# Routing of a mixture of experts: rows for the gathers made behind the choice of experts, a second index list moved forward, weights' high parts cast earlier

## The chip, the cores and the metric

The kernel runs on one core of one Trainium2 chip, in one launch. The metric is the time of one execution on the device in microseconds (us); less is better. A core has five engines that work side by side, each through its own instructions in order: TensorE (PE in the profile, with its weight loads as PEld), VectorE (DVE), ScalarE (ACT), GpSimd (POOL) and SyncE (SP), which here only issues DMA transfers. They wait for each other through semaphores.

## The reference

One decoder layer on 512 tokens of 1024 channels. An attention and a recurrent mixer come first; then a mixture of 16 experts, which is where the change lies:

```python
u = layer_norm(x) * (1.0 + sc_f) + sh_f
grp_prob = softmax(t @ w_grp + b_grp)              # 4 groups, top 1
sel_logits = ...                                   # 4 experts of that group
top_w, top_idx = top_k(softmax(sel_logits), 2)     # top 2
...
for e in range(16):
    h = silu(t @ w_e_gate[e]) * (t @ w_e_up[e])
    y = y + comb[:, e:e + 1] * (h @ w_e_down[e])
x = layer_norm(alpha * x + (1.0 + gt_f) * y, ln2_g, ln2_b)
```

All is float32. `t` is `u` with one row for each token.

## The kernel before, in words

**Blocks.** The 512 tokens are four blocks of 128 (t = 0 to 3). Each block's attention output is projected (`out_half`, L938, in halves h: `oh(t, h)` is its products, `oe(t, h)` its addition to x on DVE, L945) and goes through two layer norms, `out_ln` (L969), in five steps `L[t][0..4]`:

- `L[t][0]`: mean on DVE (L951), squares on ACT (L957), one scaling pass on DVE in two halves (L978), the reciprocal root on POOL (L962, L326).
- `L[t][1]`: the pass with that root (L984), which gives x of the next residual.
- `L[t][2]`: mean, squares and root of the second norm.
- `L[t][3]`: u2's first pass, (x + mean) × scale row, two DVE instructions on 128x512 (L994).
- `L[t][4]`: u2's second pass, × root + shift row (L998), and on POOL's queue the DMA that writes the block's rows to `u2d` in device memory (L999). Experts gather their tokens from there.

**Logits.** They don't need u2. `RT[t]` (L1005) transposes x on PE, `RE[t]` (L1010) copies it out on ACT, `RL[t]` (L1030) multiplies by the folded routing weights (L1034), and `RN[t]` (L1037) applies both roots on DVE (L1040, L1041). `SX[t]` (L1017) scales x on ACT and writes it to `x2d` by a DMA on ACT's queue.

**Choice and positions.** `R[0]` to `R[2]` (L1189 to L1208) choose the group, the first and the second expert in small DVE steps over all four blocks. `R[3]` (L1210) makes the mask `mkb` (L1212), counts every token's place in its expert by small products on PE, and makes `posb` (L1219). `R[4]` counts each expert's tokens. `OR`, `PT`, `SP_` and `PP` (L1266, L1559 to L1570) order the experts by load; the order goes to SP for the later weight loads.

**The first expert.** Its tokens are not gathered: `FO` (L1536) makes a one-hot matrix `oh0` from `posb`, `FM(t)` (L1540) multiplies block t of u2 with it on PE, sixteen 128x128 products in the trace, and `FX` (L1551) splits the sum into a high and a low part, cast on ACT (L97) and subtracted on DVE (L98). `IX[p]` (L1525, L1359) makes another expert's index list, by a one-hot on DVE (L1379) and a product with it on PE (L1317), and starts its gather on POOL's queue (L1333).

**Parts.** An expert's weights come in twelve tiles of 512 KB, four each of gate, up and down. For experts with over 64 places each tile is split: high part by a cast on ACT (L811), low part by a subtraction on DVE or, for every second tile of four, POOL (L812). Three products (L101 to L103) stand for one. `e_half` (L1466) does the gate or the up half, 24 products of 128x512. `pre_split(g)` (L1162) splits the first expert's gate tile g ahead of that. There are four pairs of buffers for high and low parts.

**Idle work.** `K(n)` (L1119) and `KR(name, n)` (L1127) issue n products on PE whose result nobody reads; a `KR` waits for the tile named. Each float32 product of this sort is two records in the trace.

**Order.** `TAIL` (L39) is a list written out by hand. Each entry issues its instructions on all engines it uses, so the list is the order of every engine's queue in this stretch. What follows the list is ordered by the framework's scheduler, which may let it pass steps of the list on DVE, ACT and POOL; PE's and SP's order is always the written one. `ahead(n)` (L1060) issues n weight loads on SP's queue. Such a load waits until its buffer is free; eight of these buffers hold the four blocks of x and the rows g1, b1, scf and shf before, so they come free with `SX` and with the last uses in `L[t][0]`, `L[t][1]`, `L[t][3]` and `L[t][4]`.

Of the kernel before, what the change touches and what calls it, by code (L numbers as in the profile page):

```python
# [8 lines left out]
F32 = mybir.dt.float32  # L9
# [10 lines left out]
S = 512  # L20
# [27 lines left out]
def block_kernel(ctx, tc, x, c, w_ada, b_ada, w_in, b_f, conv_w, conv_b, w_rg, b_rg, w_ig, b_ig,  # L48
# [3 lines left out]
    V, A, G, T, SP = nc.vector, nc.scalar, nc.gpsimd, nc.tensor, nc.sync  # L52
# [654 lines left out]
    FR = [fold_shift, fold_scale(scfT), fold_mean, fold_b1, fold_scale(vt[:, 0:8]), fold_mean]  # L707
# [34 lines left out]
    def GW(n, k, eng):  # L742
        return lambda: eng.tensor_mul(st["wo" + n][k], st["wo" + n][k], gtm)
# [50 lines left out]
    wq = {}  # L794
# [14 lines left out]
    def e_split(r, eng=None):  # L809
        hl = hilo(list(r.shape))  # L810
        A.copy(hl[0], r)  # L811
        (eng or V).tensor_sub(hl[1], r, hl[0].bitcast(F32))  # L812
        return hl
# [246 lines left out]
    def ahead(n):  # L1060
        return lambda: load_next(n)
# [7 lines left out]
    L = {t: out_ln(t) for t in range(NT)}  # L1069
    SS = [lambda t=t: att_ss(t) for t in range(NT)]  # L1070
# [48 lines left out]
    def K(n):  # L1119
        def f_():  # L1120
            p = ps([128, 128])
            for _ in range(n):
                T.matmul(p, ident, ident, start=True, stop=True)
# [14 lines left out]
    E5 = ahead(NRW)  # L1138
# [740 lines left out]
```

## Time and profile before

| | us |
|---|---|
| median of 3 runs | 660.27 |
| lowest and highest | 658.4, 661.78 |
| profiled execution | 662.26 |
| its span, first to last instruction | 660.6 |
| PE busy in it | 601.3 |
| DVE, ACT, POOL busy | 459.8, 322.5, 187.7 |

The profile has one execution. A row of a timeline reads: start, duration of the stretch, engine, line, operation, what it writes and reads, the shapes, how many instructions were merged, and in brackets how long the engine had been idle and whose result ended that. A row of the table by stretch has the stretch, its length, busy time and number of instructions of PE, PEld, DVE, ACT and POOL, then the granted share of TensorE's clock (1.00 is full), the DMA engines' share and GB/s. Times count from the span's start. The routing lies between about 285 and 321 us; the experts follow, and a last layer norm from 626 on.

### The profile page before, as it was taken

How to read it: one execution, taken by the hardware profiler on the slowest of the kernel's cores; microseconds unless marked ns; L12 is line 12 of the kernel's file. 1: busy time of each engine (PE TensorE's matmuls, PEld its weight loads, DVE VectorE, ACT ScalarE, POOL GpSimd, SP SyncE). 2: the span in 40 equal slices, each digit the busy share in tenths (PEclk: the TensorE clock that was granted, in tenths of full speed). 3: DMA queues.
4: the chain of work that ended last, by engine and by line, in shares of the span. 5: the costliest groups of instructions: out<-in, count | busy, mean ns of one | idle time of the engine just before them, and what ended most of it. 6: DMA issues, size and time to landing. Idle time of an engine off the chain costs nothing. (4 is left out here: it accounts for less than half of the span.)

```text
span 660.6 us, 10240 instructions
## 1 busy us (share of the span) xinstructions
PE 601.3 (91%) x3545; PEld 442.5 (67%) x3545; DVE 459.8 (70%) x739; ACT 322.5 (49%) x508; POOL 187.7 (28%) x191
## 2 busy tenths in 40 slices
PE   4898999999999999989799999999999999999960
PEld 0556868767886888879577776566767677676440
DVE  6757879844655677896789577747677685985185
ACT  0444887343444465742666455345536364552170
POOL 8700004000000000330255334344436344443023
PEclk9899999999999999987989999999999899999885
DMA  9996045977367123556699969799989999699503
GB/s 314 342 261 219 5 160 183 292 232 223 96 222 262 60 70 122 200 214 223 205 362 382 376 207 381 233 350 332 353 280 370 369 377 360 224 388 384 203 18 113
DMA packets 90578, 164.61 MB, mean 249 GB/s; under 512 B 9321, under 2 KB 29913, under 8 KB 90524
## 3 DMA queue, kind: packets, MB, share of 16 engines
q1 hardware_dynamic: 83796, 149.02, 64.6%
q0 software_dynamic: 5024, 10.70, 6.2%
q10 hardware_dynamic: 1704, 4.21, 1.7%
q8 instruction: 29, 0.48, 0.3%
q14 instruction: 25, 0.20, 0.1%
HBM read 155.54 MB, written 12.39 MB: 254 GB/s over the span
## 5 line engine op out<-in xcount | busy, mean ns | idle before, releaser
L812 DVE TENSOR_TENSOR wlo<-er,whi 128x1024 fp32r<-128x1024 f32 x91 | 145.1, 1612 | 31.6 <-ACT whi L811 30.0
L811 ACT CAST whi<-er 128x1024 fp32r<-128x1024 f32 x120 | 125.3, 1049 | 73.3 <-PE ps L103 64.2
L812 POOL TENSOR_TENSOR wlo<-er,whi 128x1024 fp32r<-128x1024 f32 x29 | 74.3, 2563 | 78.5 <-ACT whi L811 78.3
L101 PE MATMUL ps<-uh,whi 128*128 128x512 f32 x160 | 64.4, 403 | 0.0
L102 PE MATMUL ps<-wlo,xth 128*128 128x512 f32 x144 | 58.5, 406 | 5.7 <-POOL wlo L812 4.1
L103 PE MATMUL ps<-uh,wlo 128*128 128x512 f32 x160 | 62.6, 391 | 0.0
L102 PE MATMUL ps<-ul,whi 128*128 128x512 f32 x160 | 62.4, 390 | 0.0
L1418 PE MATMUL ps<-er,xT 128*64 128x256 f32 x512 | 60.3, 389 | 0.0
L101 PE MATMUL ps<-whi,xth 128*128 128x512 f32 x144 | 59.4, 412 | 0.0
L103 PE MATMUL ps<-whi,xtl 128*128 128x512 f32 x144 | 58.2, 404 | 1.2 <-DVE xtl L98 1.2
L1418 PEld LDWEIGHTS ps<-er,xT 128*64 128x64 f32 x512 | 36.0, 140 | 20.8 <-issue 5.0
L326 POOL TENSOR_TENSOR rA<-rA,nhalf 128x1 f32<-128x1 f32 x4 | 2.2, 548 | 157.4 <-DVE rA L917 157.4
L101 PEld LDWEIGHTS ps<-uh,whi 128*128 128x128 f32 x160 | 30.1, 188 | 11.5 <-issue 3.9
L102 PEld LDWEIGHTS ps<-wlo,xth 128*128 128x128 f32 x144 | 27.7, 192 | 13.5 <-POOL wlo L812 5.8
L358 DVE TENSOR_TENSOR wlo<-wi,whi 128x1024 fp32r<-128x1024 f32 x20 | 25.5, 1277 | 15.3 <-ACT whi L357 15.3
L357 ACT CAST whi<-wi 128x1024 fp32r<-128x1024 f32 x20 | 21.0, 1048 | 28.8 <-DMA wi<-in_w_in_dram 17.0
L103 PEld LDWEIGHTS ps<-uh,wlo 128*128 128x128 f32 x160 | 30.0, 188 | 6.9 <-DVE wlo L358 0.5
L102 PEld LDWEIGHTS ps<-ul,whi 128*128 128x128 f32 x160 | 30.1, 188 | 6.4 <-issue 0.5
L102 PE MATMUL ps<-wlo,hth 128*128 128x512 f32 x80 | 31.9, 398 | 2.5 <-DVE wlo L812 2.5
L103 PEld LDWEIGHTS ps<-whi,xtl 128*128 128x128 f32 x144 | 27.9, 194 | 8.1 <-DVE xtl L98 1.6
L101 PE MATMUL ps<-whi,hth 128*128 128x512 f32 x80 | 32.4, 405 | 0.0
L101 PEld LDWEIGHTS ps<-whi,xth 128*128 128x128 f32 x144 | 27.9, 194 | 5.8
(416 smaller groups left out, 1266.5 us busy)
## 6 DMA issues: line engine op xcount, KB each, us to landing
er<-in_w_e_gate_dram SPq DMA_DIRECT2D x64, 512.0 KB, 8.2
er<-in_w_e_up_dram SPq DMA_DIRECT2D x64, 512.0 KB, 10.6
er<-in_w_e_down_dram SPq DMA_DIRECT2D x64, 512.0 KB, 10.9
wa<-in_w_ada_dram SPq DMA_DIRECT2D x44, 512.0 KB, 8.6
wi<-in_w_in_dram SPq DMA_DIRECT2D x20, 512.0 KB, 4.9
wo<-in_w_out_dram SPq DMA_DIRECT2D x8, 512.0 KB, 5.0
wa<-in_w_ada_dram ACTq DMA_DIRECT2D x4, 512.0 KB
x<-in_x_dram SPq DMA_DIRECT2D x4, 512.0 KB, 6.0
```

The costliest lines, as they stand in the source:

```text
L101: T.matmul(o, l[0], r[0], start=start, stop=False)
L102: T.matmul(o, l[0], r[1], start=False, stop=False)
L103: T.matmul(o, l[1], r[0], start=False, stop=stop)
L326: G.tensor_tensor(dst, src, nhalf[:, 0:n], op=OP.pow)
L357: A.copy(hl[0], r)
L358: V.tensor_sub(hl[1], r, hl[0].bitcast(F32))
L811: A.copy(hl[0], r)
L812: (eng or V).tensor_sub(hl[1], r, hl[0].bitcast(F32))
L1418: T.matmul(p[64 * h:64 * h + 64, :], xT[:, k, :], ws[w0 + k // 2][:, k % 2, h * 256:(h + 1) * 256], start=k == 0, stop=k == 7)
```

## The change

Nothing is computed differently; the list is reordered, `pre_split` is cut in two, and the idle products are redistributed.

- `L[3][4]`, `L[2][3]`, `L[1][3]` and `L[0][3]` move: the first from before `RT[1]` to between `R[2]` and `R[3]`, the others to behind `FO`, each shortly in front of its own second pass.
- `RE[0]` moves in front of `L[1][2]`, `SX[2]` behind `SP_`.
- `K(10)` becomes `K(6)` in front of `RT[0]` and `K(6)` behind `L[0][2]`; `KR` 5 and 5 become 3 and 2.
- `IX[1]` moves from behind `FX` to in front of `FM(0)`.
- `pre_split(g)` becomes `PA(g)`, the cast on ACT, and `PB(g)`, the subtraction on DVE. `PA(0)` to `PA(2)` go among the choice and the positions, `PA(3)` in front of `FX`; `PB(0)` in front of `FM(0)`, the others behind `FX`.
- `SX[1]` and `SX[0]`, which stood in front of the weights `WM`, go to the very end.

The list from the first difference on, broken into lines here:

```diff
-    RN[3], L[3][4], oh(0, 0), RT[1], RE[1], L[1][1], L[2][3], oh(0, 1), RL[2], oe(0, 0), oe(0, 1), L[0][0],
-    RT[0], RL[1], L[1][2], RE[0], RN[2], L[1][3], L[0][1], RL[0], L[0][2], K(10), SX[3], RN[1], L[0][3], SX[2], RN[0],
-    ahead(3), R[0], KR("em", 5), R[1], KR("oh1", 5), R[2], R[3], FO, L[2][4], R[4], FM(3), IX[0], OR, FM(2), L[1][4],
-    PT, SP_, FM(1), L[0][4], PP, FM(0), pre_split(0), FX, IX[1], pre_split(1), SX[1], SX[0], WM, pre_split(2), pre_split(3),
+    RN[3], oh(0, 0), RT[1], RE[1], L[1][1], oh(0, 1), RL[2], oe(0, 0), oe(0, 1), L[0][0], K(6),
+    RT[0], RL[1], RE[0], L[1][2], RN[2], L[0][1], RL[0], L[0][2], K(6), SX[3], RN[1], RN[0], PA(0),
+    ahead(3), R[0], KR("em", 3), PA(1), R[1], KR("oh1", 2), R[2], L[3][4], R[3], FO, L[2][3], R[4], FM(3), L[2][4], IX[0], OR,
+    PA(2), FM(2), L[1][3], L[1][4], PT, SP_, SX[2], FM(1), L[0][3], L[0][4], PP, IX[1], PB(0), FM(0), PA(3),
+    FX, PB(1), PB(2), WM, PB(3), SX[1], SX[0],
```
```diff
-    def pre_split(g):
-        return lambda: hl0.append(e_split(wq[0][g]))
+    def PA(g):
+        def f_():
+            hl0.append(hilo(list(wq[0][g].shape)))
+            A.copy(hl0[g][0], wq[0][g])
+        return f_
+
+    def PB(g):
+        return lambda: V.tensor_sub(hl0[g][1], wq[0][g], hl0[g][0].bitcast(F32))
```

More of the change, by code (lines that the diff above doesn't have):

```diff
@@ L39, in TAIL @@
 def TAIL(d):
-    (S_, N_, T_, PV_, oh, oe, lo, L, SS, RT, RE, RL, RN, FR, FO, FM, FX, AL, AC, G, V, K, KR, SX, open_e1, open_e3, ahead, pre_split, pj, w_ahead, AU, LW, GW, FW, XA, E5, RW, scsh_rows, R, IX, OR, PT, SP_, PP, WM) = (d[k] for k in ("S_", "N_", "T_", "PV_", "oh", "oe", "lo", "L", "SS", "RT", "RE", "RL", "RN", "FR", "FO", "FM", "FX", "AL", "AC", "G", "V", "K", "KR", "SX", "open_e1", "open_e3", "ahead", "pre_split", "pj", "w_ahead", "AU", "LW", "GW", "FW", "XA", "E5", "RW", "scsh_rows", "R", "IX", "OR", "PT", "SP_", "PP", "WM"))
+    (S_, N_, T_, PV_, oh, oe, lo, L, SS, RT, RE, RL, RN, FR, FO, FM, FX, AL, AC, G, V, K, KR, SX, open_e1, open_e3, ahead, PA, PB, pj, w_ahead, AU, LW, GW, FW, XA, E5, RW, scsh_rows, R, IX, OR, PT, SP_, PP, WM) = (d[k] for k in ("S_", "N_", "T_", "PV_", "oh", "oe", "lo", "L", "SS", "RT", "RE", "RL", "RN", "FR", "FO", "FM", "FX", "AL", "AC", "G", "V", "K", "KR", "SX", "open_e1", "open_e3", "ahead", "PA", "PB", "pj", "w_ahead", "AU", "LW", "GW", "FW", "XA", "E5", "RW", "scsh_rows", "R", "IX", "OR", "PT", "SP_", "PP", "WM"))
@@ L41, in TAIL @@
     S, N, T, PV, le = S_, N_, T_, PV_, oe
     return [
-        AL, AL, pj(1, 0), AC, AC, AL, AL, pj(1, 1), AC, AC, T[0], S[1], N[1], AU[6], pj(2, 0), LW["L"], AL, GW("L", 0, V), GW("L", 1, V), FW["L"][0], pj(2, 1), AL, T[1], PV[0], S[2], AU[7], N[2], AC, AC, FW["L"][1], GW("L", 2, V), AL, pj(3, 0), AU[8], FW["L"][2], GW("L", 3, V), AL, pj(3, 1), AC, AC, AU[9], open_e1, T[2], S[3], N[3], PV[1], S[4], FW["L"][3], AL, AL, AL, AL, PV[2], T[3], N[4], RW[0], lo(0, 1), AC, AC, PV[3], LW["A"], scsh_rows, FR[0], FR[1], XA[0], XA[2], lo(0, 0), AC, AC, GW("A", 0, V), lo(1, 0), FR[2], le(0, 0), le(0, 1), XA[1], S[5], T[4], N[5], GW("A", 1, V), S[6], lo(2, 1), PV[4], RW[1], FR[3], FR[4], lo(2, 0), GW("A", 2, V), GW("A", 3, V), le(1, 0), AU[10], lo(1, 1), FR[5], le(1, 1), XA[3], S[7], T[5], N[6], SS[3], le(2, 1), S[8], PV[5], lo(3, 0), T[6], N[7], le(2, 0), AU[11], lo(3, 1), FW["A"][0], FW["A"][1], FW["A"][2], FW["A"][3], le(3, 0), T[7], E5, N[8], PV[6], S[9], le(3, 1), oh(3, 0), oh(3, 1), T[8], oe(3, 0), PV[7], N[9], S[10], T[9], N[10], PV[8], oe(3, 1), SS[2], oh(2, 1), oh(2, 0), L[3][0], T[10], RT[3], oe(2, 0), RE[3], PV[9], L[3][1], PV[10], RL[3], SS[1], oe(2, 1), open_e3, ahead(4), oh(1, 0), L[3][2], L[2][0], SS[0], RT[2], RE[2], L[3][3], L[2][1], oh(1, 1), oe(1, 0), oe(1, 1), L[2][2], L[1][0], RN[3], L[3][4], oh(0, 0), RT[1], RE[1], L[1][1], L[2][3], oh(0, 1), RL[2], oe(0, 0), oe(0, 1), L[0][0], RT[0], RL[1], L[1][2], RE[0], RN[2], L[1][3], L[0][1], RL[0], L[0][2], K(10), SX[3], RN[1], L[0][3], SX[2], RN[0], ahead(3), R[0], KR("em", 5), R[1], KR("oh1", 5), R[2], R[3], FO, L[2][4], R[4], FM(3), IX[0], OR, FM(2), L[1][4], PT, SP_, FM(1), L[0][4], PP, FM(0), pre_split(0), FX, IX[1], pre_split(1), SX[1], SX[0], WM, pre_split(2), pre_split(3),
@@ new lines, in TAIL @@
+        AL, AL, pj(1, 0), AC, AC, AL, AL, pj(1, 1), AC, AC, T[0], S[1], N[1], AU[6], pj(2, 0), LW["L"], AL, GW("L", 0, V), GW("L", 1, V), FW["L"][0], pj(2, 1), AL, T[1], PV[0], S[2], AU[7], N[2], AC, AC, FW["L"][1], GW("L", 2, V), AL, pj(3, 0), AU[8], FW["L"][2], GW("L", 3, V), AL, pj(3, 1), AC, AC, AU[9], open_e1, T[2], S[3], N[3], PV[1], S[4], FW["L"][3], AL, AL, AL, AL, PV[2], T[3], N[4], RW[0], lo(0, 1), AC, AC, PV[3], LW["A"], scsh_rows, FR[0], FR[1], XA[0], XA[2], lo(0, 0), AC, AC, GW("A", 0, V), lo(1, 0), FR[2], le(0, 0), le(0, 1), XA[1], S[5], T[4], N[5], GW("A", 1, V), S[6], lo(2, 1), PV[4], RW[1], FR[3], FR[4], lo(2, 0), GW("A", 2, V), GW("A", 3, V), le(1, 0), AU[10], lo(1, 1), FR[5], le(1, 1), XA[3], S[7], T[5], N[6], SS[3], le(2, 1), S[8], PV[5], lo(3, 0), T[6], N[7], le(2, 0), AU[11], lo(3, 1), FW["A"][0], FW["A"][1], FW["A"][2], FW["A"][3], le(3, 0), T[7], E5, N[8], PV[6], S[9], le(3, 1), oh(3, 0), oh(3, 1), T[8], oe(3, 0), PV[7], N[9], S[10], T[9], N[10], PV[8], oe(3, 1), SS[2], oh(2, 1), oh(2, 0), L[3][0], T[10], RT[3], oe(2, 0), RE[3], PV[9], L[3][1], PV[10], RL[3], SS[1], oe(2, 1), open_e3, ahead(4), oh(1, 0), L[3][2], L[2][0], SS[0], RT[2], RE[2], L[3][3], L[2][1], oh(1, 1), oe(1, 0), oe(1, 1), L[2][2], L[1][0], RN[3], oh(0, 0), RT[1], RE[1], L[1][1], oh(0, 1), RL[2], oe(0, 0), oe(0, 1), L[0][0], K(6), RT[0], RL[1], RE[0], L[1][2], RN[2], L[0][1], RL[0], L[0][2], K(6), SX[3], RN[1], RN[0], PA(0), ahead(3), R[0], KR("em", 3), PA(1), R[1], KR("oh1", 2), R[2], L[3][4], R[3], FO, L[2][3], R[4], FM(3), L[2][4], IX[0], OR, PA(2), FM(2), L[1][3], L[1][4], PT, SP_, SX[2], FM(1), L[0][3], L[0][4], PP, IX[1], PB(0), FM(0), PA(3), FX, PB(1), PB(2), WM, PB(3), SX[1], SX[0],
```

## The prediction

> **What bounds the kernel now.** I read the page first, then a table of busy time by stretch, then each engine's timeline between 285 and 336 us, which is all that the change touches.
>
> ```profile
> span 660.6 us, 10240 instructions
> ...
> PE 601.3 (91%) x3545; PEld 442.5 (67%) x3545; DVE 459.8 (70%) x739; ACT 322.5 (49%) x508; POOL 187.7 (28%) x191
> ```
> ```profile
> sum 335.00, PE 300.80 PEld 210.88 DVE 233.57 ACT 164.47 POOL 136.36; mean PE 18.80 PEld 13.18 DVE 14.60 ACT 10.28 POOL 8.52
> ```
>
> From 326 us on PE is busy 300.8 of 335.0 us, and the last 35 of these are the closing normalisation. The experts are PE work, so what the routing stretch in front of them gives up should reach the end nearly whole. That stretch is a chain of short steps:
>
> ```profile
> 288.37 0.75 DVE L984 SCALAR_TENSOR_TENSOR xt<-xg,rs,b 128x512 f32<-128x512 f32 x1 [0.44 <-POOL rs L326]
> ...
> 289.72 1.41 DVE L994 SCALAR_TENSOR_TENSOR u<-xt,nmu,scf 128x512 f32<-128x512 f32 x2
> 291.05 0.74 DVE L945 SCALAR_TENSOR_TENSOR xt<-ps,rA,xt 128x512 f32<-128x512 f32 x1
> ...
> 294.63 1.41 DVE L994 SCALAR_TENSOR_TENSOR u<-xt,nmu,scf 128x512 f32<-128x512 f32 x2
> 295.96 0.75 DVE L984 SCALAR_TENSOR_TENSOR xt<-xg,rs,b 128x512 f32<-128x512 f32 x1
> ...
> 300.37 0.24 DVE L1040 SCALAR_TENSOR_TENSOR lg<-ps,rs,b1w 128x20 f32<-128x20 f32 x1 [0.92 <-PE ps L1034]
> 300.72 0.24 DVE L1041 SCALAR_TENSOR_TENSOR lg<-lg,rs,brow 128x20 f32<-128x20 f32 x1
> ...
> 305.11 0.22 DVE L1212 TENSOR_TENSOR mkb<-e1o,e2o 128x64 bf16<-128x64 f32 x1
> 307.95 0.23 DVE L1219 SCALAR_TENSOR_TENSOR posb<-ps,mkb 128x64 bf16<-128x64 f32 x1 [2.62 <-PE ps L1217]
> 308.21 0.69 DVE L1538 TENSOR_TENSOR oh<-iota1b,posb 128x512 f32<-128x512 bf16 x1
> ```
> ```profile
> 287.82 1.85 PE L1034 MATMUL ps<-wr,yT 128*128 128x20 f32 x16
> 291.85 1.83 PE L1008 MATMUL ps<-ident,xt 128*128 128x128 f32 x8 [2.18 <-DVE xt L945]
> 293.48 6.86 PE L1034 MATMUL ps<-wr,yT 128*128 128x20 f32 x32
> 300.17 4.61 PE L1123 MATMUL ps<-ident 128*128 128x128 f32 x20
> ...
> 307.50 0.21 PE L1215 MATMUL ps<-mkb,utrib 128*128 128x16 bf16 x2
> ...
> 315.75 1.06 PE L1297 MATMUL ps<-pm,sT 16*128 16x16 f32 x8
> 316.74 2.05 PE L1548 MATMUL ps<-oh,u 128*128 128x128 f32 x16
> 320.79 0.35 PE L1317 MATMUL ps<-cidx,oh 128*128 128x1 bf16 x8 [2.00 <-DVE oh L1379]
> 321.00 0.48 PE L101 MATMUL ps<-whi,x0h 128*128 128x512 f32 x1
> ...
> 330.36 0.48 PE L101 MATMUL ps<-whi,x0h 128*128 128x512 f32 x1
> ...
> 335.79 0.40 PE L103 MATMUL ps<-whi,x0l 128*128 128x512 f32 x1
> ```
> ```profile
> 293.00:295.00 2.00, 2.00 (x12) 2.00 (x11) 1.96 (x6) 1.65 (x3) 0.74 (x2) 0.50 0.00 0
> ```
>
> See first the clock. Sixteen logit products took 1.85 us (0.116 each) at 288, thirty-two took 6.86 us (0.214 each) at 293: after PE's 2.18 us pause the granted clock is 0.50 (last row, third column from the end). The ten unused products of K (20 records) run at that clock too, 0.23 us each, and keep PE's queue full until 307.5: posb waits 2.62 us behind them, although mkb is there at 305.33.
>
> **The change part by part.** *The passes ahead of the choice.* Four pairs of L994/L998 leave DVE. Block 3's L998 frees nothing: the next step waited 0.44 us for POOL already. Block 2's L994 stood right in front of the last output halves: 291.05 − 289.72 = 1.33 us. Block 1's L994 stood in front of block 0's second step, whose POOL root was there at 294.98:
>
> ```profile
> 294.42 0.56 POOL L326 TENSOR_TENSOR rs<-vs,nhalf 128x1 f32<-128x1 f32 x1
> ...
> 299.58 0.55 POOL L326 TENSOR_TENSOR rs<-vs,nhalf 128x1 f32<-128x1 f32 x1
> ```
>
> so it cost 295.96 − 294.98, about 0.9. Block 0's L994 lay in front of a wait for PE: nothing. The last logits need L1041, which needs the root at 300.13 and ran at 300.72, because L1040 had waited for slow PE products. The new K(6) stands between products that end at 289.67 and transposes that can start near 290.5: twelve records of 0.13 (2.05/16) are 1.5 us, so PE doesn't pause, and the logits keep 0.116. Then the root is what ends last: 0.5 more. Sum 1.33 + 0.9 + 0.5 = 2.7: the choice begins at 298.3 instead of 301.0. If the clock falls all the same, the two sets of products from about 293.0 end at 299.9 and only 0.4 is left. I take 2.7, as K fills the pause that stands in front of the fall.
>
> *The choice and the positions.* From 300.96 to mkb at 305.11 is 4.1 us of small steps; block 3's L998 now stands in front of mkb, 1.33: mkb at 303.7, done 303.9. The product itself takes 307.95 − 307.50 = 0.45, and PE is now free for it, since K's second half ends near 297.5 (first K to 291.2, transposes about 1.1, twice 1.85, second K 1.5) and KR's ten records are short. posb at 304.4 instead of 307.95: 3.5 gained.
>
> *From the positions to the first product.* Six passes now lie here that lay ahead.
>
> ```profile
> 311.30 0.14 DVE L1268 COPY cntT<-ps 16x1 f32<-16x1 f32 x1
> ...
> 312.17 1.39 DVE L998 SCALAR_TENSOR_TENSOR u<-u,rs,shf 128x512 f32<-128x512 f32 x2
> ...
> 316.85 0.22 DVE L1568 CAST posb<-ps 128x56 bf16<-128x56 f32 x1 [1.48 <-PE ps L1297]
> ...
> 319.16 0.23 DVE L1365 TENSOR_SCALAR posc<-posP 128x4 bf16<-128x4 f32 x2
> 319.44 0.69 DVE L98 TENSOR_TENSOR x0l<-ps,x0h 128x512 fp32r<-128x512 f32 x1
> ...
> 322.45 0.17 DVE L1233 TENSOR_TENSOR gd<-lg,gm 128x16 f32<-128x16 f32 x1
> ...
> 325.86 3.49 DVE L812 TENSOR_TENSOR wlo<-er,whi 128x1024 fp32r<-128x1024 f32 x3
> ```
>
> DVE in order from 304.4: posb and oh0 0.9 (305.3), block 2's two passes 2.7 (308.0), the order of experts 312.17 − 311.30 = 0.9 and an index 0.1 (309.0), block 1's two passes 2.7 (311.7). PE: FM(1) 2.05 (313.8), by-position products and their wait 316.85 − 315.75 = 1.1 (314.9; block 0's two passes, 311.8 to 314.5, hide beside these), two casts 0.4, the second one-hot 0.7 (316.0), its product 0.35, FM(0) 2.05 (318.4). The first product follows at 318.5, not 321.0, as its second index list no longer stands in front with a 2.00 us wait: 2.5.
>
> But the new order leaves PE nearly empty: from 297.5 to 305.4 it has KR's ten records (1.3 us) and the positions (0.5), less than in the stretch in front of the fall at 292. I take the clock as halved when FM(3) begins. FM(3) then needs 4.1 instead of 2.05 (305.4 to 309.5), its index 0.7; if dense work has raised the clock by then, FM(2) ends at 312.2, transposes and spread take 0.8, FM(1) ends at 315.1, and the first product comes at 319.8: 1.2 gained. The Trainium skill (TensorE: Matmul & The Clock Gate, Part 1) has the clock halved after an idle window of about 3.4 us. By it the longest gap here, 2.5 us (301.4 to 303.9), would not halve it and the sum would take 318.5; the trace differs, since 2.18 us between thin products was enough.
>
> *High and low parts.*
>
> ```profile
> 320.25 1.06 ACT L1018 ACTIVATE xt<-xt 128x1024 f32<-128x1024 f32 x1
> ...
> 323.87 0.22 ACT L1235 ACTIVATE gx<-gd 128x16 f32<-128x16 f32 x1 [1.09 <-issue]
> ...
> 324.50 3.87 ACT L811 CAST whi<-er 128x1024 fp32r<-128x1024 f32 x4
> ```
> ```profile
> 328.46 3.14 POOL L812 TENSOR_TENSOR wlo<-er,whi 128x1024 fp32r<-128x1024 f32 x1 [4.94 <-ACT whi L811]
> ```
>
> The four casts (0.97 each) go to times when ACT is idle: free. The first gate half took 321.0 to 330.0, 24 products at 0.236 ((335.79 − 330.36)/23) being 5.7; the rest is waiting for parts. Now the last low part ends it. FX's last subtraction ends 320.13 − 318.79 = 1.3 behind FM(0); two low parts at 1.16 are 2.3; the weights took 325.86 − 322.45 = 3.4, of which 1.1 was ACT busy with x's stores, so 2.3; the last low part 1.2. From FM(0)'s end (319.7 with the halved clock) that makes 326.8, five products 1.2 more: 328.0 instead of 330.0. With the clock full, 326.7.
>
> Then the up half. x's last two stores (3.6 us of ACT, 320.25 to 323.87) now stand behind the weights. Casts of the up weights, issued behind the written order, can pass them: L1365 at 319.16 belongs to a later expert and runs between two steps of the list. If the first two pass, the up half follows at 328.3 and ends 5.7 later at 334.0, against 336.2: **2.2 us gained**, the forecast. If they don't, that is the second rival.
>
> *DMAs.* Block 2's store of x goes out near 312.8, not 301.8, and the rows used as scf and shf come free at 313 and 314.5.
>
> ```profile
> 305.26 10.47 SPq L819 DMA_DIRECT2D er<-in_w_e_down_dram  x3
> ```
> ```profile
> x2d<-xt ACTq DMA_DIRECT2D x4, 512.0 KB, 6.1
> ```
>
> These three slots take the second expert's down weights, issued from 305.3 to 315.7, now near 319 (312.8 + 6.1). They are used five blocks of 24 products behind the first: over 28 us of cover, so nothing; without it, 3 us. The gather of the second list gets its list earlier and waits for block 0's rows at 314.5: nothing. The new wait of PB(0) on DVE has only FX queued behind it, and its cast is long done.
>
> **The rivals.** *Clock kept:* if the KR products hold the clock through, the first product is at 318.5, the gate half ends at 326.7 and the up half near 332.7: 3.5 gained, 656.8. For: six KR records at 299.5 split the gap. Against: the fall at 292. The Trainium skill's page named above gives this case.
>
> *Stores in front of the up casts:* with the written order strict, ACT ends the weights' exponentials near 324.9, the stores at 328.5, the casts at 329.5 and 330.6; POOL's low part takes 3.14 (333.7), and the 17 products behind it 4.0: 337.7, 1.5 later than now, 661.8. It decides once the up casts lie behind both stores.
>
> *Clock down through all one-hot products:* the slower case by more than noise. Four FM at 4.1 with double-length products between them end about 8 us later than counted with the clock full, so the gate half ends near 335, 5 us later than now: 665. It needs three dense FM at half clock without a rise; K raised it in about 3.4 dense us (302.3 to 305.7).
>
> *No effect:* the logits' chain bound by PE anyway (0.4 instead of 2.7) while the stores cost what the earlier parts gain: 660.3.
>
> **How the numbers follow.** The profiled execution took 662.26 us (span 660.6); 2.2 less is 660.1. The median of the runs, 660.27, stands 2.0 below it, so I forecast 658.1. Chances: forecast 0.42, clock kept 0.30, stores in front 0.13, no effect 0.06, clock down 0.09. A measurement of this kernel can tell 0.5% (3.3 us) from no change. The runs before spread over 3.4 us, so a case's median can lie a microsecond or two off. Clock kept, 3.5 us, counts two thirds as faster (0.20), the forecast a third (0.14); clock down is slower (0.09), the rest within: faster 0.34, same 0.57, slower 0.09. The range, 654.8 to 662.0, takes in clock kept with 2 us of spread and the stores' case, and leaves clock down out.
>
> **What would show it.** Choice (L1191) near 298.3; posb near 304.4; first product of the experts between 318.5 and 319.8; the granted clock 0.50 somewhere between 299 and 309; the last gate low part near 326; the first two up casts on ACT ahead of x's last store. Wrong if L1034 still takes 0.21 us each behind K(6), if FM(2) and FM(1) take over 4 us, or if the gain up to the up half's end isn't that of the end.

## The result and the profile after

| | changed kernel | kernel before, beside it | ratio (95% interval) |
|---|---|---|---|
| first comparison, 4 runs each | 668.20 (665.57 to 671.01) | 661.02 (658.4 to 662.54) | 1.0131 (1.0084 to 1.0178) |
| again, as a0 below, 12 runs | 667.56 (665.52 to 669.93) | 660.52 | 1.0095 (1.0064 to 1.0127) |

Medians in us; the ratio is worked out from the single runs and is not the quotient of the medians, from which it can differ by some 0.3%. In the ratios, here and below, runs over 1.5% above the fastest of their kernel are left out (of the kernels below one of e9's, 1490.65 us, and two of f3's, 662.75 and 663.23), while the medians have them in. The change makes the kernel about 1% slower: by a0's twelve runs 7.0 us by the medians and 6.3 by the ratio, where 2.2 us of gain were forecast and the range ended at 662.0.

The profiled execution took 671.01 us. Its page begins:

```profile
span 669.3 us, 10225 instructions
...
PE 603.7 (90%) x3539; PEld 443.7 (66%) x3539; DVE 460.0 (69%) x739; ACT 322.5 (48%) x508; POOL 181.5 (27%) x191
```

PE is busy 2.4 us longer than before, the span is 8.7 us longer: PE mostly waits more.

To lay two kernels beside each other, a point upstream of the change is needed. The ninth load of expert weights on SP's queue serves, first in the kernel before, then in the changed one:

```profile
270.95 2.09 SPq L819 DMA_DIRECT2D er<-in_w_e_gate_dram  x4
```
```profile
272.95 0.46 SPq L819 DMA_DIRECT2D er<-in_w_e_gate_dram  x1
```

So 2.0 us of the 8.7 arose ahead of the change, in code that is the same (in a0, the same kernel once more, this point lies at 270.60), and times called "aligned" below have the difference of this point taken off. VectorE's timeline of the changed kernel, through choice and positions (the choice's first step, the positions):

```profile
299.67 0.17 DVE L1198 TENSOR_REDUCE gm<-lg 128x4 f32<-128x16 f32 x1
...
305.74 0.22 DVE L1226 SCALAR_TENSOR_TENSOR posb<-ps,mkb 128x64 bf16<-128x64 f32 x1 [0.53 <-PE ps L1224]
```

The choice begins at 297.7 aligned and posb at 303.7, 4.2 us earlier than before; posb waits 0.53 us for its product instead of 2.62. TensorE's timeline from the logits to the up half:

```profile
293.80 3.65 PE L1034 MATMUL ps<-wr,yT 128*128 128x20 f32 x32
...
306.75 3.78 PE L1555 MATMUL ps<-oh,u 128*128 128x128 f32 x16 [0.76 <-DVE oh L1545]
...
310.58 2.48 PE L1555 MATMUL ps<-oh,u 128*128 128x128 f32 x16
...
318.06 0.35 PE L1324 MATMUL ps<-cidx,oh 128*128 128x1 bf16 x8 [1.21 <-DVE oh L1386]
318.27 3.66 PE L1555 MATMUL ps<-oh,u 128*128 128x128 f32 x16
321.61 0.55 PE L101 MATMUL ps<-whi,x0h 128*128 128x512 f32 x1
...
332.05 0.79 PE L102 MATMUL ps<-wlo,x0h 128*128 128x512 f32 x1 [4.52 <-DVE wlo L1170]
...
335.29 0.54 PE L101 MATMUL ps<-whi,x0h 128*128 128x512 f32 x1
```

The logits keep 0.114 us each (3.65/32). The first expert product starts at 319.6 aligned, 1.4 us earlier than before. Then the gate half stops for 4.52 us for its last low part (L1170, `PB(3)`), and takes 12.9 us instead of 8.95; the up half begins 2.9 us later than before, aligned. The table by stretch has the granted clock in its third column from the end:

```profile
288.00:297.00 9.00, 9.00 (x75) 8.65 (x73) 7.01 (x22) 5.30 (x10) 2.65 (x7) 1.00 0.28 98
...
297.90:311.50 13.60, 9.64 (x65) 8.62 (x64) 9.90 (x36) 5.05 (x7) 2.03 (x5) 0.50 0.47 177
318.40:321.70 3.30, 3.30 (x18) 3.30 (x17) 2.00 (x3) 0.59 (x1) 0.00 (x0) 0.50 0.96 233
332.10:335.40 3.30, 3.30 (x18) 2.27 (x18) 2.73 (x6) 0.00 (x0) 0.00 (x0) 0.50 0.47 159
```

The clock is halved three times here: through the positions and FM(3), in FM(0), and in the gate half's last five products. Why the last low part is late stands in VectorE's timeline, with POOL's row for the same time:

```profile
325.47 0.17 DVE L1240 TENSOR_TENSOR gd<-lg,gm 128x16 f32<-128x16 f32 x1
...
327.13 2.59 DVE L1250 TENSOR_SCALAR den<-dd 128x4 f32<-128x4 f32 x1 [0.74 <-ACT dd L1248]
...
330.63 0.23 DVE L1259 TENSOR_TENSOR wm<-wm,w 128x64 f32<-128x64 f32 x1
330.78 1.22 DVE L1170 TENSOR_TENSOR wlo<-er,whi 128x1024 fp32r<-128x1024 f32 x1
```
```profile
327.31 2.37 POOL L812 TENSOR_TENSOR wlo<-er,whi 128x1024 fp32r<-128x1024 f32 x1
```

The softmax weights (WM, L1240 to L1259) take 5.3 us. One of their steps, on 128x4, takes 2.59 us; it starts 0.2 us before POOL begins the low part of the second up tile, and ends with it. That tile's high part came early, because ACT's casts for the up half passed x's stores.

One expert later nearly all of this is given back, since the kernel before loses time there that the changed one doesn't. VectorE's, POOL's and TensorE's rows of the kernel before, behind the first expert's up half:

```profile
336.87 2.79 DVE L812 TENSOR_TENSOR wlo<-er,whi 128x1024 fp32r<-128x1024 f32 x1
```
```profile
335.52 3.06 POOL L812 TENSOR_TENSOR wlo<-er,whi 128x1024 fp32r<-128x1024 f32 x1
```
```profile
340.32 0.79 PE L103 MATMUL ps<-whi,xtl 128*128 128x512 f32 x1 [1.21 <-DVE xtl L98]
```

DVE's pass takes 2.79 us instead of 1.22 beside POOL's, xtl comes late behind it, and the clock is halved from 339.83 to 343.24: the second expert's gate half takes 8.63 us before and 5.85 after. Its up half begins at 347.58 before and at 347.78 aligned after, so of the 3.0 us that the first expert's up half ends later 0.2 are left in this pair of profiles. The half-clock window there is not in every profile: in e2 below, with the routing of the kernel before, the half takes 6.59 us and the up half begins at 346.68 aligned, which would leave 1.1.

A second loss lies far off, at the last expert with 128 rows, 280 us behind the edit. ACT's timeline there, before and after:

```profile
591.14 1.05 ACT L811 CAST whi<-er 128x1024 fp32r<-128x1024 f32 x1 [1.83 <-PE ps L103]
599.53 0.58 ACT L97 CAST hth<-ps 128x512 fp32r<-128x512 f32 x1 [7.34 <-PE ps L1499]
600.01 1.05 ACT L811 CAST whi<-er 128x1024 fp32r<-128x1024 f32 x1
600.96 0.39 ACT L1486 ACTIVATE sg<-ps 128x256 f32<-128x256 f32 x1
601.24 1.99 ACT L811 CAST whi<-er 128x1024 fp32r<-128x1024 f32 x2
603.78 0.59 ACT L1401 COPY xT<-ps 128x512 f32<-128x512 f32 x1 [0.55 <-PE ps L1400]
```
```profile
603.05 0.59 ACT L97 CAST hth<-ps 128x512 fp32r<-128x512 f32 x1 [10.23 <-PE ps L1506]
603.53 0.39 ACT L1493 ACTIVATE sg<-ps 128x256 f32<-128x256 f32 x1
607.30 0.59 ACT L1408 COPY xT<-ps 128x512 f32<-128x512 f32 x1 [3.38 <-PE ps L1407]
607.78 3.89 ACT L811 CAST whi<-er 128x1024 fp32r<-128x1024 f32 x4
```

Before, ACT casts the four down tiles ahead of the copy xT; after, all four stand behind it, and the copy waits for PE. PE then waits for each part in turn:

```profile
608.88 0.50 PE L101 MATMUL ps<-whi,hth 128*128 128x512 f32 x1 [1.62 <-ACT whi L811]
610.14 0.50 PE L102 MATMUL ps<-wlo,hth 128*128 128x512 f32 x1 [0.76 <-DVE wlo L812]
...
612.39 0.50 PE L102 MATMUL ps<-wlo,hth 128*128 128x512 f32 x1 [0.59 <-POOL wlo L812]
```

The down half takes 7.73 instead of 5.85 us and starts some 1.7 us later behind the products before it: 3.6 us. Another 1.7 us follow there, as the half-clock window behind this expert is 6.83 us long instead of 3.41, and 1.3 arose between the two experts, with one more such window. No entry that the change moved is executed there. It is the order that the scheduler gave ACT and DVE that differs.

### The profile page after: what moved, and what is told of

It reads as the page before. It is cut to its first block, busy times and chain, and to the rows that moved or that the text cites. A ratio compares the mean times of both kernels' runs of the same rounds, so it can differ in the third digit from the quotient of the medians.

```text
span 669.3 us, 10225 instructions
## 1 busy us (share of the span) xinstructions
PE 603.7 (90%) x3539; PEld 443.7 (66%) x3539; DVE 460.0 (69%) x739; ACT 322.5 (48%) x508; POOL 181.5 (27%) x191
## 4 chain that ended last, share of the span: by engine, by line
PE 68%; DVE 11%; DMA 10%; issue 4%; ACT 3%; POOL 2%; ACTq 0%; SPq 0%; DVEq 0%; POOLq 0%
PE ps L102 14%; PE ps L101 14%; PE ps L103 14%; PE ps L1425 7%; DMA er<-in_w_e_down_dram 3%; PE ps L1441 3%; DMA er<-in_w_e_gate_dram 2%; DVE wlo L812 2%; DMA wa<-in_w_ada_dram 2%; DMA er<-in_w_e_up_dram 2%; PE ps L290 2%; DMA wi<-in_w_in_dram 1%; DVE tail L1760 1%; PE ps L883 1%; PE ps L1555 1%
## 5 line engine op out<-in xcount | busy, mean ns | idle before, releaser
L812 DVE TENSOR_TENSOR wlo<-er,whi 128x1024 fp32r<-128x1024 f32 x87 | 136.0, 1580 | 32.9 <-ACT whi L811 32.9
L811 ACT CAST whi<-er 128x1024 fp32r<-128x1024 f32 x116 | 121.2, 1049 | 68.2 <-PE ps L103 60.6
L812 POOL TENSOR_TENSOR wlo<-er,whi 128x1024 fp32r<-128x1024 f32 x29 | 72.7, 2507 | 85.0 <-ACT whi L811 84.8
L103 PE MATMUL ps<-whi,htl 128*128 128x512 f32 x80 | 32.1, 401 | 0.0
```

The costliest lines, as they stand in the source:

```text
L103: T.matmul(o, l[1], r[0], start=False, stop=stop)
```

## The experiments

Three theories were set against each other: the end's order (A), the routing stretch with its clock (B), and the collision of DVE and POOL in the first expert (D). All sixteen kernels are timed against the kernel before, in four sets (e1 to e4; a0, e8, e9 and e10; the f's; the h's), each with the kernel before beside it and with twelve runs of a kernel, eight of h4: medians compare within a set, ratios also across sets. Times in the table are aligned; "gate half" is the first expert's, "down half" that of the last expert with 128 rows; each comes from the one profiled execution of that kernel.

| kernel | median | ratio (95% interval) | posb | first product | gate half | up half's end | down half |
|---|---|---|---|---|---|---|---|
| before | 660.1 to 662.1 | 1 | 307.95 | 321.01 | 8.95 | 336.19 | 5.85 |
| a0, the change | 667.56 | 1.0095 (1.0064 to 1.0127) | 303.77 | 319.69 | 13.05 | 339.27 | 7.72 |
| e1 | 664.49 | 1.0034 (1.0006 to 1.0061) | 303.74 | 319.48 | 13.03 | 339.25 | 7.82 |
| e2 | 664.43 | 1.0063 (1.0032 to 1.0094) | 308.13 | 321.19 | 9.91 | 337.33 | 7.73 |
| e3 | 664.79 | 1.0063 (1.0035 to 1.0090) | 303.72 | 319.51 | 7.09 | 340.77 | 9.35 |
| e4 | 660.77 | 0.9995 (0.9967 to 1.0024) | 303.78 | 319.28 | 9.43 | 334.95 | 7.82 |
| e8 | 662.32 | 1.0016 (0.9983 to 1.0049) | 303.73 | 319.27 | 12.47 | 338.90 | 5.85 |
| e9 | 658.81 | 0.9974 (0.9936 to 1.0013) | 303.75 | 319.18 | 10.53 | 336.34 | 5.85 |
| e10 | 661.05 | 0.9991 (0.9958 to 1.0024) | 303.73 | 319.35 | 7.11 | 332.36 | 5.85 |
| f1 | 659.40 | 0.9974 (0.9940 to 1.0009) | 306.57 | 319.62 | 8.26 | 334.11 | 5.85 |
| f2 | 657.36 | 0.9940 (0.9913 to 0.9967) | 307.23 | 320.08 | 9.32 | 335.63 | 5.84 |
| f3 | 659.66 | 0.9967 (0.9930 to 1.0005) | 303.75 | 319.06 | 8.25 | 333.55 | 5.85 |
| f4 | 660.92 | 1.0004 (0.9974 to 1.0034) | 307.97 | 321.03 | 8.25 | 335.50 | 5.85 |
| h3 | 658.41 | 0.9976 (0.9946 to 1.0006) | 303.76 | 319.19 | 9.76 | 335.18 | 5.85 |
| h1 | 665.35 | 1.0054 (1.0023 to 1.0085) | 303.74 | 316.61 | 12.93 | 336.11 | 5.85 |
| h2 | 661.60 | 1.0010 (0.9980 to 1.0040) | 304.94 | 316.31 | 12.93 | 336.02 | 5.85 |
| h4 | 655.37 | 0.9914 (0.9878 to 0.9950) | 304.97 | 316.34 | 9.33 | 332.10 | 5.85 |

**e1, one edge at the end.** An order edge without a semaphore:

```diff
                 hl = e_split(wq[p][8 + k], G if k in PG else None)
+                if p == SEQ[13] and k == 2:
+                    tc.add_manual_dep(st["xcp"].ins, st["cast"].ins.name, NOSYNC, reason="order")
```

> The changed kernel, with one edge added: the copy of the transposed block (xT, L1408) is issued on ACT behind the third cast of the last 128-row expert's down tiles, as ACT had it in the kernel before. Nothing else moves. Theory A (most of the loss is made near the end, where ACT's order changed 280 us behind the edit): the down half of that expert ends 3.6 us earlier than in the changed kernel, without the three idles of 1.62, 0.76 and 0.59 us, and the time falls from 668.2 by 3.6 to about 664.6 (ratio to before 1.005), or by up to 5 if the half-clock window behind it shrinks back from 6.83 to 3.41 us. Rival B (the loss comes from the routing stretch and from the clock): no change, 668 (ratio 1.013).

The wait of 1.62 us in front of the down half went, but the half itself kept its length, as one low part was now late:

```profile
605.75 0.50 PE L103 MATMUL ps<-wlo,hth 128*128 128x512 f32 x1 [1.70 <-DVE wlo L813]
```

On DVE it stood behind sg's product, which waits for PE, and beside a pass of POOL. The ratio, 1.0034, was smaller than theory A gave (1.005): against the 1.0131 of the first comparison that would be 6 us for one edge, so the change itself was measured again.

**a0, the change again.**

> The changed kernel as it is, in as many rounds as the experiments, since its own median (668.2) came from four runs and e1, meant to change only its end, came out at ratio 1.0034. If e1 differs from it by the end's order (theory A), its ratio is e1's plus 1.6 to 2.0 us (down half 7.7 us in both, first product of it 1.6 us later in the changed kernel): 1.006 to 1.007; if the four runs were fair, 1.013.

1.0095: between the two expected values. The first comparison's value was somewhat high, though the intervals overlap.

**e2, the wrong order in the kernel before.** The first cast of those down tiles behind xT; nothing of the routing is touched.

> The kernel before, with one edge added: the first cast of the last 128-row expert's down tiles is issued on ACT behind the copy xT, the order of the changed kernel. Routing as before. Theory A: 3.6 us slower than before, about 664.6 (ratio 1.005), or up to 666 with a longer half-clock window behind it; the down half shows idles of about 1.6, 0.8 and 0.6 us for the parts of its weights. Rival B: no change, 661 (ratio 1.000).

Slower than before by 0.63%, 4.2 us (2.4 by the medians), with the three waits of the changed kernel (1.62, 0.76 and 0.61 us) and its 7.73 us. The order alone costs about what theory A says.

**e8, the whole order put back.** Four casts, hth, sg and xT on ACT, and the low parts on DVE, in the order of the kernel before:

```diff
+                if p == SEQ[13]:
+                    es = st["es"]
+                    if k == 0:
+                        behind(st["ht"][0], es[0])
+                        behind(st["ht"][1], es[1])
...
+                    if k == 3:
+                        behind(st["xcp"], es[0])
```

> The changed kernel with the whole order of the kernel before put back at the last 128-row expert's down tiles: on ACT first cast, hth, second cast, sg, third and fourth cast, xT copy; on DVE the first low part ahead of htl and the third ahead of the product of sg. (e1 had only put the xT copy behind the third cast; its down half still took 7.81 us, 603.55 to 611.36, with a wait of 1.70 us for a low part.) Theory A: down half 5.85 us as before, no wait in it over 0.3 us, 2 us less than e1: ratio near 1.000. Rival: the wait of 1.70 us moves to the next expert's halves and the ratio stays at 1.003.

The down half is back at 5.85 us, without a wait:

```profile
602.54 0.50 PE L101 MATMUL ps<-whi,hth 128*128 128x512 f32 x1
```

667.56 − 662.32 = 5.2 us less than a0, which was timed beside it (0.0079 by the ratios, the same 5.2): most of the loss. The timelines account for 3.6 of it. A half-clock window behind this expert was 6.83 us long in the profiles of the changed kernel, a0 and e2 and 3.41 in that of e8, which would be 1.7 more; but it is 6.83 in e9 too. And between 345 and 600 us, where every engine's order is the same in both kernels, e8's profile is 4.7 us shorter than a0's, which has two half-clock windows there (at 513.96 and 537.85) where e8's has none. So one pair of profiles can't place the rest, and that part stays open.

**e4, the low part on DVE.** With e1's edge:

```diff
-                hl = hl0[g] if (p, w0) == (0, 0) and g < len(hl0) else e_split(wq[p][w0 + g], G if g in PG else None)
+                hl = hl0[g] if (p, w0) == (0, 0) and g < len(hl0) else e_split(wq[p][w0 + g], G if g in PG and (p, w0) != (0, 4) else None)
```

> e1 with the low part of the second up tile of the first expert on DVE instead of POOL, so that no long POOL pass runs while DVE makes the softmax weights WM. Theory D (DVE's small steps stretch from 0.17 to 2.59 us while POOL runs its 2.4 us pass of 128x1024): WM takes about 2.8 us on DVE instead of 5.3, no step of 128x4 takes over 0.3 us, and the first gate half ends 2.5 us earlier. Rival E (the 2.59 us were a wait for data that the profile counts as busy): WM's step stays near 2.6 us. The time: as e1 if the first expert's gains are given back, up to 2.5 us less if they aren't.

VectorE's timeline of e4:

```profile
327.95 0.17 DVE L1251 TENSOR_SCALAR den<-dd 128x4 f32<-128x4 f32 x1 [0.72 <-ACT dd L1249]
...
329.18 1.22 DVE L1171 TENSOR_TENSOR wlo<-er,whi 128x1024 fp32r<-128x1024 f32 x1
```

The step takes 0.17 us, WM 2.9 (326.31 to 329.18) instead of 5.3, the gate half 9.43 instead of 13.03; the up half ends 4.3 us earlier. The time is 3.7 us less than e1's by the medians, 2.6 by the ratios. Theory D holds. Between these two kernels the second expert gives nothing back, as its gate half waits in neither (5.82 us in both): most of the gain reached the end.

**e9, both repairs.**

> e8 and e4 together: the end's order put back, and the second up tile's low part of the first expert on DVE. e4 alone gave 0.9995, 3.7 us less than e1, with the first gate half at 9.43 instead of 13.03 us. If both losses are separate and both reach the end, 2 us less than e4: ratio 0.996 to 0.997, 658.8. If what is won at one place is given back at the other, as e4: 0.9995.

3.5 us less than e8 by the medians, 2.8 by the ratios; 1.4 less than e4 by the ratios. So each repair reads about the same with the other as without it, and the two losses look separate, though the intervals of e8, e4 and e9 overlap. Without the losses the change is no longer slower than the kernel before.

**e3, PB(3) in front of WM.** With e1's edge: `PB(1), PB(2), PB(3), WM`.

> e1 with the last gate low part, PB(3), in front of the experts' softmax weights WM on DVE. Theory A with give-back (the second expert's gate half waits for its block's low part xtl in any case, so time lost or won in the first expert does not reach the end): the first gate half ends about 4 us earlier than in the changed kernel (near 328.5 with the offset of 2.0 us taken off), and the time is that of e1 within 1 us, ratio 1.005. Rival C (what the first expert wins reaches the end): about 4 us less than e1, 660.6 (ratio 0.999).

The gate half took only 7.09 us, but the next products on PE are the transposes of the softmax weights, and WM was later still, with the collision in another of its steps:

```profile
328.43 2.73 DVE L1248 TENSOR_TENSOR dd<-m,m 128x4 f32<-128x4 f32 x1
```
```profile
335.73 1.01 PE L1297 MATMUL ps<-ident,wm 128*16 128x128 f32 x4 [5.79 <-DVE wm L1260]
```

The wait moved from one side of WM to the other. Theory A had the time (0.3 us from e1 by the medians, 1.9 by the ratios) for another reason than it gives: the up half ends 1.5 us later than e1's, so nothing was won that could have been given back, and rival C isn't tested by it either.

**e10, the transposes behind the up half.** e9, PB(3) in front of WM, and `wmT = by_expert(wm)` moved.

> e9 with PB(3) in front of WM, and the transposes of the softmax weights (by_expert(wm)) issued on PE behind the first expert's up half instead of between its gate half and its up half, so that neither half waits for WM. Theory F (WM on the path was what PB(3) and the transposes waited for: 2.09 us in e4's gate half, 5.79 us behind e3's): gate half about 7.1 us as in e3, up half straight behind it, some 2 us less than e9: ratio 0.993 to 0.994. Rival G (the up tiles' parts are late next, since ACT casts the third and fourth up tile only behind x's stores): the up half waits by what the gate half wins, ratio as e9.

Theory F was right on the halves (7.11 us, then straight on; the up half ends 4.0 us earlier than e9's) and wrong on the time, 0.9991. In its profile the second expert's gate half begins only 5.0 us behind the up half, instead of 2.2, and its first products then run half-clocked, until 343.50:

```profile
337.40 1.06 PE L1306 MATMUL ps<-pm,sT 16*128 16x16 f32 x8 [0.75 <-ACT sT L1300]
...
342.20 0.63 PE L102 MATMUL ps<-wlo,xth 128*128 128x512 f32 x1
```

A product of 0.63 us takes 0.39 at full clock. The gain went into the transposes now in front of this half, three small waits (0.75, 0.92 and 0.38 us) and a half-clock window of 3.41 us that begins as the third ends.

**f1, the control.** The kernel before, with the low part on DVE.

> The control for e9: the kernel before (its routing list untouched, its end's order pinned as it is) with the second up tile's low part of the first expert on DVE instead of POOL. Theory H (that low part costs only where it lies beside the softmax weights; in the kernel before it lies behind them, at 328.46): no change, ratio 1.000 within 0.002, and e9's 0.9974 is what the change itself is worth, about 1.7 us, once its two side effects are taken away. Rival I (POOL's 3.14 us pass is late in the kernel before too, and e9's gain is that of the repair): ratio 0.996 to 0.997.

0.9974, the value of e9. Theory H is not confirmed: the repair seems to help the kernel before as well (its interval takes in 1), and what the change itself is worth, with the repairs in both, is nothing that these runs can tell. The trace of the kernel before speaks against H too. POOL's 3.14 us there are in DVE's way, if not in that of the softmax weights; a low part of 1.22 us takes 3.01 beside them:

```profile
329.68 3.01 DVE L812 TENSOR_TENSOR wlo<-er,whi 128x1024 fp32r<-128x1024 f32 x1 [0.33 <-ACT whi L811]
```

**f3, passes alone; f4, parts alone.** Both with the repairs.

> Only the first part of the change, with e9's two repairs: the passes of three blocks behind the choice and the unused products as in the changed kernel; second index list and high and low parts where they were. By the prediction's steps the positions come 3.5 us earlier (posb near 304.4 instead of 307.95), but FM(3) and FM(0) run at half clock and the wait of 2.00 us for the second index list stays: first expert product 0 to 1 us earlier than before, and the gate half's parts at the earliest when x's blocks let ACT go: ratio 0.998 to 1.000. Rival: the earlier positions reach the end by 2 us or more, 0.997 or less.

> Only the last part of the change, with e9's two repairs: high parts (PA), low parts (PB) and x's last two stores placed as in the changed kernel, passes, unused products and second index list as in the kernel before. By the prediction's steps the first product stays at 321.0 (offset of the run taken off), and the gate half takes 8 to 9.4 us (as e4, 9.43) instead of 8.95; the up half follows with its first casts already made: ratio 0.997 to 1.000. Rival: the parts' order is what loses, since it puts WM in front of PB(3): gate half over 9.5 us, ratio over 1.002.

Passes alone: 0.9967, with the up half ending 2.6 us earlier than before in the profile. The value is the rival's, its interval takes in both (with the two runs that the ratio leaves out it is some 0.998), and f1 has 0.9974 without the passes. Parts alone: 1.0004, about as expected. In f3 the second index list stands behind FM(0) and PE waits 2.00 us for it, as before:

```profile
316.77 2.05 PE L1565 MATMUL ps<-oh,u 128*128 128x128 f32 x16
320.83 0.35 PE L1319 MATMUL ps<-cidx,oh 128*128 128x1 bf16 x8 [2.00 <-DVE oh L1381]
```

Yet its first expert product is no later than the changed kernel's (319.06 against 319.69), and 1.9 us earlier than before, where 0 to 1 was expected: FM(0) ran at full clock.

**h3, the index list behind FM(0) again.** e9 but for that.

> e9 (changed kernel with both repairs) with the second index list back behind FM(0) and FX, where the kernel before has it. In the changed kernel it stands in front of FM(0): PE waits there for DVE, the clock falls again (half at 316.3 with the run's offset taken off) and FM(0) runs 316.3 to 319.6 instead of the 314.8 to 316.9 that f3 shows. Theory J (that early list costs what it saves): first product near 319.1 instead of 319.2, but x's parts 2.8 us earlier, so the gate half takes 1 to 2 us less than e9's and ends near 327.5; ratio 0.994 to 0.996. Rival K (the list's place is neutral, e9's lack of gain lies elsewhere): first product up to 2 us later than e9 with the same gate half, ratio 0.997 to 1.000.

0.9976, first product 319.19: the list's place is neutral, as rival K has it for the time, though not for the first product, which didn't come later. In front of FM(0) the list waits 1.21 us for DVE and FM(0) runs at half clock (3.66 us); behind it, in h3, the wait is 2.00 us and FM(0) takes 2.05.

**f2, more unused products.** e9 with `KR("em", 12)` and `KR("oh1", 14)`.

> e9 with 12 and 14 unused products instead of 3 and 2 in the stretch between the choice and the positions, so that PE has some 3 us more to do there. Clock theory (the granted clock falls at 298 because PE is nearly idle there): it stays at 1.0 through the one-hot products, FM(3) takes 2.05 instead of 3.8 us and FM(0) 2.05 instead of 3.7, the first expert product comes 1.2 to 3 us earlier than in e9 and the ratio is 0.993 to 0.995. Rival: such thin products don't hold the clock; it falls all the same, the added records run at 0.23 us and stand in front of the positions: ratio 0.997 to 1.002.

The clock came back earlier, at 303.0 aligned (306.1 as read, the offset being 3.05) instead of 309.5:

```profile
299.30:305.90 6.60, 5.01 (x24) 4.72 (x24) 5.00 (x22) 3.18 (x5) 0.74 (x2) 0.50 0.62 228
306.10:311.20 5.10, 4.43 (x53) 4.13 (x51) 1.09 (x5) 0.00 (x0) 0.69 (x1) 1.00 0.26 105
```

All four FM ran in 2.05 us or less. But the added products stood in front of the positions (posb 307.23), and the first expert product came later, at 320.08. The ratio is 0.994, as the clock theory gave it, though nothing was won where it said; e9's interval overlaps, and where the difference lies these profiles don't show.

**h1, the list behind the gate half; h2, that with 12 and 4 unused products.** Both on f3.

> f3 (passes behind the choice alone, both repairs) with the second index list issued on PE behind the first gate half, ahead of the third list. Its gather waits on POOL for the stores of u until about 326 in e4, so nothing needs the list at 319. Theory L (the first product waits only for the list, 316.85 to 319.06 in f3): first product near 317.5, gate half 8.3 to 9.0, up half's end near 332.5 instead of 333.55; ratio 0.9945 to 0.9965, f3 having 0.9967. Rival M (the low parts set the gate half's end, as DVE is the late one): the gate half ends as in f3, near 327.3, ratio as f3.

> h1 with 12 and 4 unused products instead of 3 and 2 (f2 had 12 and 14: the clock rose at 303.0 instead of 309.5, but the 14 stood in front of the positions until 306.9). Clock theory: half-clock window ends near 303, positions near 304.5, FM(3) 2.05 us; one-hot chain 2 us shorter than in h1; ratio 0.991 to 0.994. Rival: without the fourteen the clock stays down through FM(3) as in h1, ratio as h1.

The first product came at 316.6 and 316.3, so only the list had held it. But high and low parts, made where the kernel before makes them, were now late, and the gate half took 12.93 us, with the clock halved in its pauses. h1's waits:

```profile
323.19 0.50 PE L102 MATMUL ps<-wlo,x0h 128*128 128x512 f32 x1 [1.02 <-DVE wlo L814]
...
327.71 0.79 PE L102 MATMUL ps<-wlo,x0h 128*128 128x512 f32 x1 [1.01 <-DVE wlo L814]
...
341.69 1.06 PE L1411 MATMUL ps<-ident,xg 128*128 128x128 f32 x8 [2.35 <-DMA xg<-u2d,ix]
```

The last row is the price of the late list: the gather lands late. In h1, L was right on the first product and wrong on what follows; M had the low parts late, but not that they cost 4.7 us. In h2 the clock came back as the clock theory has it, and FM(3) took 2.05 us; but the twelve products stood in front of the positions (posb 304.94 against 303.74), so the first product gained 0.3 us and not 2.

**h4, the same with the change's early parts.** The whole change, the list behind the first gate half, 12 and 4 unused products, both repairs.

> e9 with the second index list behind the first gate half and 12 and 4 unused products: the whole change but for the list's place, with both repairs and the clock kept. Theory J: as h2 or better by the 0.5 us that the earlier high parts give, ratio 0.990 to 0.994. Rival (PB(3) behind WM costs about 2 us of waiting in the gate half, 2.09 us in e9): 1 to 2 us more than h2, ratio 0.994 to 0.996.

0.9914 (0.9878 to 0.9950), the fastest here, and faster than the kernel before and the changed one. Every FM takes 2.05 us, the first product is at 316.34, the gate half takes 9.33 us, of which the wait for PB(3) behind WM is still 2.08; the wait for the gather is down to 0.39 us:

```profile
328.84 0.50 PE L102 MATMUL ps<-wlo,x0h 128*128 128x512 f32 x1 [2.08 <-DVE wlo L1172]
```

The number is theory J's, but partly by luck: J had h2 there too, which measured 1.0010, and gave the early parts 0.5 us. Beside h2 the profile shows what they are worth once the products come early: 3.6 us of the gate half. In f4, where the products come as late as before, the same parts are worth nothing that can be told (1.0004).

## Why the prediction was wrong

- *Choice and positions*: right. The choice at 297.7 (298.3 forecast), posb at 303.7 (304.4), logits at 0.114 us behind K(6).
- *One-hot products*: right in sum, partly by luck. FM(3) 3.78 us (4.1), first product 319.6 (319.8); but FM(1) ended 1.2 us earlier than summed (313.9 for 315.1), and the stretch behind it took 5.8 us for 4.7. What the move of the second list was to save, its 2.00 us wait, it did not: h3, with the list back, starts at 319.19. The list still waited 1.21 us, and FM(0) behind it took 3.66 us at half clock. The clock was halved for FM(3) as taken, though not for the reason given: it fell at 295.9 aligned, ahead of the stretch in which PE is nearly empty.
- *Casts ahead of x's stores*: right as an event. Two up casts ran ahead of x's last two stores, a third between them. The consequence was missed.
- *High and low parts*: the step that failed first. The sum gave "1.3 + 2.3 + 2.3 + 1.2" behind FM(0) and 326.8 for the last low part. Measured, aligned: 1.4, 2.3, **5.4** and 1.2, to 330.0. The term for the softmax weights was taken from the kernel before, where POOL's pass came behind them; the hoisted cast released that pass into them. The five products behind took 2.5 instead of 1.2 us at half clock. Gate half 332.5 for 328.0. e4 takes the pass away: 328.7, and the up half ends at 334.95 for a forecast 334.0. So the rest of the sum stood within 1 us.
- *What the routing gives up should reach the end nearly whole*: the larger failure, twice. Of the 3.0 us that the first expert lost, 2.8 did not reach the second expert's up half, as the kernel before loses them there itself, to the same collision and the clock. And of the 6.3 us of a0, putting the order back at the last 128-row expert is worth 5.2 (e8; 3.6 stand in the timelines of that expert), where the sum had no term. The prediction treated all behind the list as unchanged; it is ordered by a scheduler, and the edit changed that order. e2 and e8 show this from both sides. Why the scheduler chose otherwise there, with ACT's order the same but for one cast from 355 to 590 us, was not tried and stays open.
- *DMAs*: right. The next load of weights on SP's queue came 4.4 us later (332.16 less 2.0, against 325.74), behind block 1's store of x, and the one after it 7.4 us later (338.54 less 2.0, against 329.09), as block 0's store was issued behind a copy that waited 5.70 us for PE; the second expert's gate half ran in 5.85 us all the same.
- *The rivals*: none was the case. The one that ends slower, clock down through all one-hot products, had the sign by another mechanism: FM(2) took 2.48 and FM(1) 2.05 us.
- The forecast gain of 2.2 us: with both repairs the change reads 0.9974, 1.7 us, but the control f1 reads the same. Against that control nothing is left that can be told from zero; passes alone and parts alone say likewise. Below the kernel before, clear of the noise, are only f2 (0.9940), with more unused products, and h4 (0.9914), with the list's place mended as well; whether h4's additions would do as much without the passes' move was not tried.

## What to carry to other kernels

An edit to a list written by hand ends at its last line, but a scheduler orders what follows, so compare every engine's order over the whole program before saying that the rest is unchanged. A step made earlier releases others: ask what each of them will run beside, DVE beside POOL above all. And a wait that is removed in front of one half is worth only what the next late part leaves: earlier products with the clock kept (h2, 1.001) and earlier parts (f4, 1.0004) were worth nothing alone, and 0.9% together (h4), each with the repairs, of which one reads 0.3% by itself (f1).

## What the runs showed of the hardware

*DVE stands while POOL makes a long pass, unless it reads ps.* ps are the tiles in which PE leaves its sums, in a memory of their own (PSUM); the other tiles here lie in SBUF. den (one input, 128x4) took 2.59 us and dd (two inputs, 128x4) 2.73 instead of 0.17 and 0.15. The same holds for large steps at the last expert: two passes of 1.2 us take 3.80 beside one of POOL's.

```profile
609.85 2.48 POOL L812 TENSOR_TENSOR wlo<-er,whi 128x1024 fp32r<-128x1024 f32 x1 [7.94 <-ACT whi L811]
```
```profile
610.75 3.80 DVE L812 TENSOR_TENSOR wlo<-er,whi 128x1024 fp32r<-128x1024 f32 x2 [0.67 <-ACT whi L811]
```

POOL's ends at 612.33, and 612.33 plus two of 1.2 is 614.7, near DVE's end at 614.55: the first pass hardly began until POOL was done. Steps that read ps run on, as here in the kernel before, where POOL makes a low part from 374.91 to 377.31:

```profile
375.54 1.45 DVE L1519 SCALAR_TENSOR_TENSOR y<-ps,wsl,gtf 128x512 f32<-128x512 f32 x2 [1.19 <-PE ps L103]
```

These two take 0.75 us each, as elsewhere. Over all eighteen profiles, 292 low parts that DVE began during a low part of POOL's ended 1.07 to 1.10 us behind POOL's end, and 364 steps that read ps took their usual time. POOL stands in turn: its 3.14 us at 328.46 instead of 2.4 began under a low part of DVE's that ran until 329.34. The Trainium skill (GPSIMD Engine Reference, Specifications) says that the two engines share their interfaces to SBUF and that DVE instructions with two inputs in SBUF or in a two-port mode contend. The rows agree, and give the size: the whole rest of the other engine's pass.

*The clock falls under a busy PE.* In the changed kernel PE was busy 9.00 of 9.00 us up to 297, with products 20 wide and unused ones, and the clock fell at 297.9. So it isn't PE's idle time alone, as the profile records it, that counts. Every window of half clock in these profiles is a multiple of 3.41 us long, but for the last, which the end cuts. The Trainium skill (TensorE: Matmul & The Clock Gate, Part 1) has such windows, running freely; the lengths agree, its idle window as the cause of a fall doesn't cover this one.

*The windows' phase is noise.* f1's routing is the kernel before's, instruction for instruction, and its posb came 1.4 us earlier, because its half-clock window was 10.24 us long instead of 13.65. Single profiles of these kernels differ by such steps, and the runs of one kernel spread over about 4 to 10 us.
